# Low halves of the second layer's first MLP weights by an adding DMA, and banks opened without matmuls of zeros

## The chip, the core and the metric

The kernel runs on one core of a Trainium2 chip. In the profile its engines are PE (matmuls; PEld is its weight load), DVE (element by element), ACT (activations and copies), POOL and SP, each with its own queue of instructions in order, and 16 DMA engines move the data. HBM is the large memory, SBUF the working memory of 128 partitions, PSUM the memory with eight banks that matmuls write. The metric is the device time of one execution, in microseconds (us); lower is better.

## What is computed

A trunk of two encoder layers on 256 tokens of 2048 features, all float32. Cut to what matters here:

```python
mod = silu(c) @ w_ada[l] + b_ada[l]              # six vectors: shift, scale, gate, twice
h = _rmsnorm(x) * (1.0 + sc_a) + sh_a
proj = h @ w_in[l]
...                                              # two kinds of attention
x = x + g_a * (concatenate([out_a, out_b]) @ w_o[l])
h = _rmsnorm(x) * (1.0 + sc_m) + sh_m
y = square(relu(h @ w_mlp_in[l])) @ w_mlp_out[l] # 2048 -> 8192 -> 2048
x = x + g_m * y
```

After both layers x is normed once more. The weights of the MLP are 2 x 64 MiB a layer.

## The kernel before

Activations stand with features on the partitions: 16 chunks of 128 features by 256 tokens. A product takes a weight block of 128 x 2048 (1 MiB, all 2048 contraction rows of one tile of 128 output features) and walks its 16 chunks.

**Weights in two halves.** PE's fast float32 form (F32R) keeps fewer bits than float32. So `weights` (L131) loads a block into `raw` on SP's queue (`raw`, L150, five buffers that the modulation's blocks share) and splits it, in two pieces of 1024 columns: ACT rounds `hi` from `raw` (L140), DVE makes `lo = raw - hi` (L141). The activations are split in the same way, so that a product is hi x hi + hi x lo + lo x hi: three matmuls for a chunk. `hi` and `lo` have four buffers each, that is room for two blocks. `weights` also hands out the loads and sums of the modulation (`ada_load`, `ada_sums`): a credit that grows with each block of weights says when the next of 192 modulation blocks is loaded.

**Two forms of product.** `mac` (L173) makes three matmuls of 256 columns. `wide` (L187) has the two parts of the activations side by side and makes one matmul of 512 columns with `hi` (L196) and one of 256 with `lo` (L197) for a chunk; its product is the sum of the bank's two halves, which `joined` (L740) takes: ACT copies one half (L744), DVE adds the other (L745).

**The MLP.** In each of four blocks of 2048 hidden features, `layer` (L696 to L717) makes the first product, tile pair by tile pair, and puts it through `relu2` (L748), then the second product with `update_wide`. The first 12 tiles of the first block come from `norm_then_by_k` (L532), contraction-chunk by contraction-chunk while the norm's chunks appear. In layer 1 the first product uses `wides` (L700): 4 tiles in the first block, 16 in each of the other three, 52 in all. In layer 0 it uses `pair`.

**Banks shared by two tiles.** `by_k` (L218) adds to several tiles by turns, two in a bank. `open_banks` (L209) opens each such bank with a matmul of zeros over all 512 columns (L213), and every later matmul adds. It is called for six banks at each of four norms' products and for two banks at four other places (the later part of the input projection and the start of the output projection, in both layers): 32 matmuls.

**Order.** The program is written in the order of the Python calls; a scheduler then sets the order on each engine, from its own estimate of when things are ready, and puts in the waits. A tile's buffer is given again when its readers are done.

Of the kernel before, what the change touches and what calls it, by code (L numbers as in the profile page):

```python
# [9 lines left out]
F32 = mybir.dt.float32  # L10
# [80 lines left out]

EARLY = {5: (0,), 6: (1, 2)}  # chunk pair of layer 0 -> quarters of w_d's contraction to run behind it
LEAD = 10  # modulation blocks summed ahead of the first norm
WHOLE = 6  # chunk pairs of layer 0's first product in plain float32 passes
# modulation blocks loaded per block of weights: in the two attentions (the second in two stretches),
# in the first products of a layer and in its MLP
RATE_A0, RATE_A1, RATE_A2, RATE_K, RATE_M = 1.1, 0.5, 0.7, 0.6, 0.66
FILL = "lb|0|1|2|3|r"  # setup pieces between the chunk pairs of layer 0


class Trunk:
# [27 lines left out]

# [1 line left out]
    def weights(self, src, width=2048):  # L131
        nc = self.nc
        raw = self.raw(src, width)
        out = []
        half = width // 2
        for i in range(2):
            v = raw[:, i * half : (i + 1) * half]
            hi = self.wp.tile([P, half], F32R, tag="hi", name=self.name("hi"), bufs=4)
            lo = self.wp.tile([P, half], F32R, tag="lo", name=self.name("lo"), bufs=4)
            nc.scalar.activation(hi, v, AF.Copy)  # L140
            ins = nc.vector.tensor_tensor(lo, v, hi.bitcast(F32), ALU.subtract)  # L141
            out.append((hi, lo))
        self.ada_sums(ins)
        self.credit += self.rate
        while self.credit >= 1.0 and self.ada_todo:
            self.credit -= 1.0
            self.ada_load()
        return out

    def raw(self, src, width):  # L150
        raw = self.wp.tile([P, width], F32, tag="raw", name=self.name("raw"), bufs=5)
        self.nc.sync.dma_start(raw, src)
        return raw

    def parts(self, name):
        """Room for a chunk's two parts: each, and both side by side."""
        v = self.u(name, F32R)
        return v[:, 0], v[:, 1], v.rearrange("p a b -> p (a b)")

    def split(self, val, name, wide=False):  # L160
        """[P, 2, T] as two chunks, each in two parts; wide: these side by side."""
        if not wide:
            hi, lo = self.u(name + "h", F32R), self.u(name + "l", F32R)
            self.nc.scalar.activation(hi, val, AF.Copy)
            self.nc.vector.tensor_tensor(lo, val, hi.bitcast(F32), ALU.subtract)
            return [(hi[:, i], lo[:, i]) for i in range(2)]
        out = [self.parts(name) for _ in range(2)]
        for i, (hi, lo, _) in enumerate(out):
            self.nc.scalar.activation(hi, val[:, i], AF.Copy)
            self.nc.vector.tensor_tensor(lo, val[:, i], hi.bitcast(F32), ALU.subtract)  # L170
        return out

    def mac(self, ps, w, c, m, x, first, last):  # L173
        mm = self.nc.tensor.matmul
        hi, lo = w[0][:, c : c + m], w[1][:, c : c + m]
        mm(ps, hi, x[0], start=first, stop=False)  # L176
        mm(ps, hi, x[1], start=False, stop=False)  # L177
        mm(ps, lo, x[0], start=False, stop=last)  # L178

# [6 lines left out]

    def wide(self, src, xs):  # L187
        """A feature tile; its product is the sum of the two halves of the bank."""
        ps = self.bank("ps")
        nk = len(xs)  # L190
        w = self.weights(src, nk * P)
        per = nk // 2
        mm = self.nc.tensor.matmul
        for k, (x, _, both) in enumerate(xs):
            hi, lo = (v[:, (k % per) * P : (k % per) * P + P] for v in w[k // per])
            mm(ps.rearrange("p a b -> p (a b)"), hi, both, start=k == 0, stop=False)  # L196
            mm(ps[:, 0], lo, x, start=False, stop=k == nk - 1)  # L197
        return ps

    def wides(self, srcs, xs):  # L200
        return [self.wide(src, xs) for src in srcs]

# [6 lines left out]
    def open_banks(self, n):  # L209
        """Banks of zeros, open for two tiles to add to by turns."""  # L210
        banks = [self.bank("pk") for _ in range(n)]
        for b in banks:
            self.nc.tensor.matmul(  # L213
                b.rearrange("p a b -> p (a b)"), self.zeros[:, :P], self.zeros, start=True, stop=False
            )
        return banks

    def by_k(self, banks, srcs, xs, k0, nk, n=4, whole=None):  # L218
        """Chunks from k0 of tiles that share banks in pairs; each block has n tiles of each chunk.
        Given the chunks whole, in plain float32 passes."""  # L220
        kpb = srcs[0].shape[-1] // (n * P)
        for b, src in enumerate(srcs):
            width = kpb * n * P
            if whole:
                w = [self.wp.tile([P, n * P], F32, tag=tag, name=self.name("w"), bufs=4) for tag in ("hi", "lo")]
                for i in range(kpb):
# [3 lines left out]
            for i in range(kpb):  # L230
                k = k0 + i
                for j in range(n):
                    tile = n * b + j
                    ps, last = banks[tile // 2][:, tile % 2], k == nk - 1 and tile % 2 == 1
                    c = (i * n + j) * P
                    if whole:
                        self.nc.tensor.matmul(ps, w[i][:, j * P : j * P + P], whole[i], start=False, stop=last)  # L237
                    else:
                        half = width // 2
                        self.mac(ps, w[c // half], c % half, P, xs[k], False, last)  # L240

    def tokens_by_k(self, pss, w, xs, first, last):
        """Token-major: pss[t] += x^T w for the chunks of one block."""
        mm = self.nc.tensor.matmul
# [8 lines left out]
    def small(self, src, xs, n):  # L253
        """n feature tiles, in banks of two, from one block that holds all of a short contraction."""
        w = self.weights(src)
# [14 lines left out]

# [1 line left out]
    def ada_plan(self):  # L272
# [15 lines left out]
    def ada_sums(self, after=None):  # L288
        """Sums over what has been loaded, on VectorE behind an instruction whose data came later."""
        nc = self.nc  # L290
# [32 lines left out]

# [1 line left out]
    def setup(self):  # L325
# [13 lines left out]
        nc.sync.dma_start(self.vec, io["vec"])  # L339
        self.zeros = cp.tile([P, 2 * T], F32R, name="zeros")  # L340
        nc.vector.memset(self.zeros.bitcast(F32), 0.0)
        self.eps = cp.tile([P, 1], F32, name="eps")
# [115 lines left out]

# [1 line left out]
    def sumsq(self, acc, val, alone=False):  # L460
        """Adds val^2, [P, 2, T], to the squares' sums acc; or, alone, puts it beside them."""
        nc = self.nc
# [15 lines left out]
    def rstd(self, acc, n):  # L478
        """1 / rms over n features, on every partition, from the squares' sums."""
        nc = self.nc  # L480
# [18 lines left out]
    def modulated(self, r, k, sh, sc, whole):  # L499
        """Chunks k and k + 1 of the modulated norm of x."""  # L500
        nc = self.nc
# [14 lines left out]
    def latent(self, vals, g):  # L516
        """Weighted rms norm over pairs of feature chunks, split."""
        nc = self.nc
# [13 lines left out]
    def norm_then_by_k(self, l, acc, sh, sc, src, n, nwhole, fill=(), early=()):  # L532
        """The modulated norm of x, and the first 4n feature tiles of its product, of whose
        contraction the first nwhole eighths take plain float32 passes."""
        r = self.rstd(acc, D)
# [17 lines left out]

# [1 line left out]
    def layer(self, l, acc):  # L555
# [140 lines left out]
        for fb in range(NFB):  # L696
            hid = []
            for m in range(0 if fb else 12, NK, 2):
                srcs = [io["w_m1"][l, NK * fb + m + j - 12] for j in range(2)]
                ps = self.wides(srcs, h) if l else self.pair(srcs, h)  # L700
                for b in banks:
# [38 lines left out]
    def joined(self, ps, out):  # L740
        """The sums of the halves of two banks."""
        for i in range(2):
# [10 lines left out]

# [1 line left out]
    def rope_k(self, ps):  # L755
        """Rows 0:64 are the keys, rows 64: their halves swapped; out twice, each over zeros."""
        nc = self.nc
# [23 lines left out]

# [1 line left out]
    def softmax_parts(self, s, least):  # L783
        """exp(max - (-s)) in place of the negated scores, and 1 / its row sums."""
        nc = self.nc
# [103 lines left out]

# [1 line left out]
    def run(self):  # L891
# [86 lines left out]
```

## Time and profile before

| | |
|---|---|
| median of 3 runs | 2266.11 us (2265.44 to 2266.87) |
| profiled execution, first to last instruction (span) | 2262.9 us |
| median less that span | 3.2 us |
| PE, PEld, DVE, ACT, POOL busy | 2202.6, 2018.0, 1654.4, 1110.2, 2.0 us |
| DMA | 585.67 MB, 259 GB/s over the span |

The profile is one execution, taken on the chip. Its page gives the busy time of each engine, the chain of work that ended last (followed back from the last instruction to what released it each time), groups of instructions by line with their number, mean duration and the idle time of the engine before them, and the DMA issues. The trace behind it answers further views: waits (who waited for whom), timelines and busy time in stretches ("PEclk" is the granted share of PE's clock, "DMA share" the mean busy share of the 16 DMA engines). "x104" is a count; "[1.36 <-DVE sum L745]" is idle time of the engine and what ended it. The matmuls' ends are modelled, so where PE's pace matters it is read from counts or starts.

### The profile page before, as it was taken

The page shows a single profiled execution, that of the slowest core. Times are in us where ns is not written, and L with a number is a line of the kernel's source. Part 1 is how long each engine was busy: PE and PEld are TensorE (multiplying, and loading weights), DVE is VectorE, ACT ScalarE, POOL GpSimd, SP SyncE. Part 2 cuts the span into 40 slices and gives each one's busy share as a digit, 9 for nine tenths or more (in the row PEclk, how much of TensorE's full clock was granted, in tenths as well). Part 3 has the DMA queues.
Part 4 walks back from the last instruction along what each step waited for, and adds up shares of the span by engine and source line. Part 5 has one row for each costly group of instructions (what it writes and reads, how often), then busy time and mean ns, then how long its engine had stood idle before and what let it go on. Part 6 is the DMA issues. An engine that isn't in the chain of part 4 may idle for free.

```text
span 2262.9 us, 35366 instructions
## 1 busy us (share of the span) xinstructions
PE 2202.6 (97%) x14508; PEld 2018.0 (89%) x14508; DVE 1654.4 (73%) x2224; ACT 1110.2 (49%) x1608; POOL 2.0 (0%) x10
## 2 busy tenths in 40 slices
PE   3999999999999999999999999999999999999998
PEld 2899889999899899899889998999988888888887
DVE  7889768888877877877888776666655555565565
ACT  2555664355454345345444465534635534544553
POOL 0000000000000000000000000000000000000000
PEclk8999999999999999999999999999999999999999
DMA  9988678898888888887879766664555555555552
GB/s 366 352 318 311 258 279 312 298 341 325 298 310 314 305 313 294 314 316 292 317 256 345 273 226 225 242 228 165 204 189 191 186 194 187 186 187 186 187 188 75
DMA packets 85268, 585.67 MB, mean 259 GB/s; under 512 B 9457, under 2 KB 9841, under 8 KB 20593
## 3 DMA queue, kind: packets, MB, share of 16 engines
q1 hardware_dynamic: 85106, 583.42, 70.9%
q8 instruction: 113, 1.85, 0.3%
q14 instruction: 49, 0.40, 0.0%
HBM read 581.28 MB, written 2.10 MB: 258 GB/s over the span
## 4 chain that ended last, share of the span: by engine, by line
PE 94%; DVE 3%; ACT 1%; DMA 1%; issue 1%; DVEq 0%; SPq 0%; ACTq 0%
PE ps L196 30%; PE ps L197 15%; PE ps L177 7%; PE ps L176 7%; PE ps L178 7%; PE pk L176 5%; PE pk L177 5%; PE pk L178 5%; PE pk L237 3%; DVE ada L293 1%; PE pv L251 1%; PE pv L249 1%; PE pv L250 1%; PE po L832 1%; PE psm L867 1%; PE pom L884 1%
## 5 line engine op out<-in xcount | busy, mean ns | idle before, releaser
L141 DVE TENSOR_TENSOR lo<-raw,hi 128x1024 fp32r<-128x1024 f32 (+1 forms) x728 | 861.4, 1185 | 469.9 <-ACT hi L140 468.1
L140 ACT ACTIVATE hi<-raw 128x1024 fp32r<-128x1024 f32 (+1 forms) x728 | 747.2, 1029 | 907.5 <-PE ps L196 478.0
L196 PE MATMUL ps<-hid,hi 128*128 128x512 f32 x2048 | 717.9, 395 | 0.0
L197 PE MATMUL ps<-hid,lo 128*128 128x256 f32 x2048 | 574.3, 280 | 0.0
L196 PEld LDWEIGHTS ps<-hid,hi 128*128 128x128 f32 x2048 | 383.9, 187 | 90.8 <-DVE hid L170 0.8
L293 DVE SCALAR_TENSOR_TENSOR ada<-ada,cond 128x2048 f32<-128x2048 f32 x192 | 438.0, 2284 | 8.5 <-ACT cond L337 6.8
L197 PEld LDWEIGHTS ps<-hid,lo 128*128 128x128 f32 x2048 | 387.0, 189 | 0.0
L196 PE MATMUL ps<-h,hi 128*128 128x512 f32 x832 | 292.4, 396 | 0.0
L176 PE MATMUL ps<-h,hi 128*128 128x256 f32 x1024 | 291.7, 285 | 0.0
L177 PE MATMUL ps<-h,hi 128*128 128x256 f32 x1024 | 290.5, 284 | 0.0
L178 PE MATMUL ps<-h,lo 128*128 128x256 f32 x1024 | 290.4, 284 | 0.0
L197 PE MATMUL ps<-h,lo 128*128 128x256 f32 x832 | 233.5, 281 | 0.0
L176 PE MATMUL pk<-h,hi 128*128 128x256 f32 x752 | 213.4, 288 | 3.9 <-ACT h L507 3.9
L177 PE MATMUL pk<-h,hi 128*128 128x256 f32 x752 | 214.8, 286 | 0.6 <-DVE h L508 0.6
L178 PE MATMUL pk<-h,lo 128*128 128x256 f32 x752 | 214.6, 286 | 0.0
L176 PEld LDWEIGHTS ps<-h,hi 128*128 128x128 f32 x1024 | 194.7, 190 | 0.4
L177 PEld LDWEIGHTS ps<-h,hi 128*128 128x128 f32 x1024 | 194.7, 190 | 0.4
L178 PEld LDWEIGHTS ps<-h,lo 128*128 128x128 f32 x1024 | 194.7, 190 | 0.2
L196 PEld LDWEIGHTS ps<-h,hi 128*128 128x128 f32 x832 | 156.1, 188 | 37.6
L197 PEld LDWEIGHTS ps<-h,lo 128*128 128x128 f32 x832 | 157.2, 189 | 0.0
L738 DVE SCALAR_TENSOR_TENSOR x<-ps,mod,x 128x256 f32<-128x256 f32 x224 | 108.3, 484 | 59.6 <-PE ps L197 54.9
L176 PEld LDWEIGHTS pk<-h,hi 128*128 128x128 f32 x752 | 145.3, 195 | 5.4 <-ACT h L507 5.3
(211 smaller groups left out, 2677.1 us busy)
## 6 DMA issues: line engine op xcount, KB each, us to landing
raw<-in_w_m SPq DMA_DIRECT2D x232, 1024.0 KB, 4.9
ada<-in_w_ada SPq DMA_DIRECT2D x192, 1024.0 KB, 5.1
raw<-in_w_ob SPq DMA_DIRECT2D x24, 1024.0 KB, 5.1
raw<-in_w_m SPq DMA_DIRECT2D x32, 768.0 KB, 4.5
raw<-in_w_dv SPq DMA_DIRECT2D x16, 1024.0 KB, 4.8
raw<-in_w_a SPq DMA_DIRECT2D x20, 768.0 KB, 6.4
raw<-in_w_t SPq DMA_DIRECT2D x12, 1024.0 KB, 5.0
w<-in_w_a SPq DMA_DIRECT2D x24, 384.0 KB, 5.2
```

Source lines behind the costliest of these rows:

```text
L140: nc.scalar.activation(hi, v, AF.Copy)
L141: ins = nc.vector.tensor_tensor(lo, v, hi.bitcast(F32), ALU.subtract)
L176: mm(ps, hi, x[0], start=first, stop=False)
L177: mm(ps, hi, x[1], start=False, stop=False)
L178: mm(ps, lo, x[0], start=False, stop=last)
L196: mm(ps.rearrange("p a b -> p (a b)"), hi, both, start=k == 0, stop=False)
L197: mm(ps[:, 0], lo, x, start=False, stop=k == nk - 1)
L237: self.nc.tensor.matmul(ps, w[i][:, j * P : j * P + P], whole[i], start=False, stop=last)
L249: mm(ps, xh, hi, start=first and k == 0, stop=False)
L250: mm(ps, xh, lo, start=False, stop=False)
L293: ins = nc.vector.scalar_tensor_tensor(w, w, 1.0, self.cond, ALU.mult, ALU.mult, accum_out=acc[:, i : i + 1])
L738: self.nc.vector.scalar_tensor_tensor(x, ps[i][:, j], g[:, m + i : m + i + 1], x, ALU.mult, ALU.add)
```

## The change

- Layer 1's first MLP product takes its weights from a new function, `weights_added`: ACT writes `hi` as before and, into `lo`, the negated rounded value (the same copy with scale -1); a DMA on POOL's queue then adds `raw` to `lo` in SBUF. DVE has no part in it, and the function neither grows the modulation's credit nor places its sums.
- `hi` and `lo` have six buffers each instead of four, also where `by_k` loads plain float32 blocks into them. The memory for it comes from the tile of zeros and from a smaller scratch for POOL's DMA descriptors (2048 bytes a partition).
- `open_banks` only takes banks. The first matmul of the first tile in each bank has `start=True` instead; a flag turns off the check of matmul groups that share a bank.
- Comments and docstrings go.

```diff
@@ weights
-            hi = self.wp.tile([P, half], F32R, tag="hi", name=self.name("hi"), bufs=4)
-            lo = self.wp.tile([P, half], F32R, tag="lo", name=self.name("lo"), bufs=4)
+            hi = self.wp.tile([P, half], F32R, tag="hi", name=self.name("hi"), bufs=6)
+            lo = self.wp.tile([P, half], F32R, tag="lo", name=self.name("lo"), bufs=6)
@@
+    def weights_added(self, src, width=2048):
+
+        nc = self.nc
+        raw = self.raw(src, width)
+        out = []
+        half = width // 2
+        for i in range(2):
+            v = raw[:, i * half : (i + 1) * half]
+            hi = self.wp.tile([P, half], F32R, tag="hi", name=self.name("hi"), bufs=6)
+            lo = self.wp.tile([P, half], F32R, tag="lo", name=self.name("lo"), bufs=6)
+            nc.scalar.activation(lo, v, AF.Copy, scale=-1.0)
+            nc.scalar.activation(hi, v, AF.Copy)
+            nc.gpsimd.dma_start(lo, v, accum_op=ALU.add)
+            out.append((hi, lo))
+        return out
@@ mac
-    def mac(self, ps, w, c, m, x, first, last):
+    def mac(self, ps, w, c, m, x, first, last, shared=False):
...
-        mm(ps, hi, x[0], start=first, stop=False)
+        mm(ps, hi, x[0], start=first, stop=False, skip_group_check=shared)
...
@@ wide
-        w = self.weights(src, nk * P)
+        w = (self.weights_added if added else self.weights)(src, nk * P)
@@ open_banks
-        banks = [self.bank("pk") for _ in range(n)]
-        for b in banks:
-            self.nc.tensor.matmul(
-                b.rearrange("p a b -> p (a b)"), self.zeros[:, :P], self.zeros, start=True, stop=False
-            )
-        return banks
+
+        return [self.bank("pk") for _ in range(n)]
@@ by_k
-                w = [self.wp.tile([P, n * P], F32, tag=tag, name=self.name("w"), bufs=4) for tag in ("hi", "lo")]
+                w = [self.wp.tile([P, n * P], F32, tag=tag, name=self.name("w"), bufs=6) for tag in ("hi", "lo")]
...
+                    first = k == 0 and tile % 2 == 0
...
-                        self.mac(ps, w[c // half], c % half, P, xs[k], False, last)
+                        self.mac(ps, w[c // half], c % half, P, xs[k], first, last, True)
@@ setup
-        self.zeros = cp.tile([P, 2 * T], F32R, name="zeros")
-        nc.vector.memset(self.zeros.bitcast(F32), 0.0)
@@ layer
-                ps = self.wides(srcs, h) if l else self.pair(srcs, h)
+                ps = self.wides(srcs, h, True) if l else self.pair(srcs, h)
@@ kernel
-    nc = bacc.Bacc("TRN2", target_bir_lowering=False, num_devices=1)
+    nc = bacc.Bacc("TRN2", target_bir_lowering=False, num_devices=1, dynamic_dma_scratch_size=2048)
```

More of the change, by code (lines that the diff above doesn't have):

```diff
@@ L171, in split @@
         return out
-    def mac(self, ps, w, c, m, x, first, last):
+    def mac(self, ps, w, c, m, x, first, last, shared=False):
         mm = self.nc.tensor.matmul
         hi, lo = w[0][:, c : c + m], w[1][:, c : c + m]
-        mm(ps, hi, x[0], start=first, stop=False)
-        mm(ps, hi, x[1], start=False, stop=False)
-        mm(ps, lo, x[0], start=False, stop=last)
+        mm(ps, hi, x[0], start=first, stop=False, skip_group_check=shared)
+        mm(ps, hi, x[1], start=False, stop=False, skip_group_check=shared)
+        mm(ps, lo, x[0], start=False, stop=last, skip_group_check=shared)
     def tile_cols(self, ps, src, xs, m=P):
@@ L185, in tile_cols, with wide @@
             self.mac(ps, w[k // per], (k % per) * m, m, xs[k], k == 0, k == nk - 1)
-    def wide(self, src, xs):
+    def wide(self, src, xs, added=False):
         ps = self.bank("ps")
         nk = len(xs)
-        w = self.weights(src, nk * P)
+        w = (self.weights_added if added else self.weights)(src, nk * P)
         per = nk // 2
@@ L198, in wide, with wides @@
         return ps
-    def wides(self, srcs, xs):
-        return [self.wide(src, xs) for src in srcs]
+    def wides(self, srcs, xs, added=False):
+        return [self.wide(src, xs, added) for src in srcs]
     def pair(self, srcs, xs):
@@ L235, in by_k @@
                     c = (i * n + j) * P
+                    first = k == 0 and tile % 2 == 0
                     if whole:
-                        self.nc.tensor.matmul(ps, w[i][:, j * P : j * P + P], whole[i], start=False, stop=last)
+                        self.nc.tensor.matmul(
+                            ps, w[i][:, j * P : j * P + P], whole[i], start=first, stop=last, skip_group_check=True
+                        )
                     else:
                         half = width // 2
-                        self.mac(ps, w[c // half], c % half, P, xs[k], False, last)
+                        self.mac(ps, w[c // half], c % half, P, xs[k], first, last, True)
     def tokens_by_k(self, pss, w, xs, first, last):
```

## The prediction

> **What bounds the kernel now.** I read the page first (busy time, slices, chain, groups), then TensorE's waits, then stretches of the second layer's MLP, then the timelines there. The page:
>
> ```profile
> PE 2202.6 (97%) x14508; PEld 2018.0 (89%) x14508; DVE 1654.4 (73%) x2224; ACT 1110.2 (49%) x1608; POOL 2.0 (0%) x10
> ...
> PE 94%; DVE 3%; ACT 1%; DMA 1%; issue 1%; DVEq 0%; SPq 0%; ACTq 0%
> ...
> L141 DVE TENSOR_TENSOR lo<-raw,hi 128x1024 fp32r<-128x1024 f32 (+1 forms) x728 | 861.4, 1185 | 469.9 <-ACT hi L140 468.1
> ```
>
> PE is busy 97% of the span of 2262.9 us and is 94% of the chain. DVE's subtractions, part of which the change removes, are the costliest group, but they are DVE's and DVE is 3% of the chain. PE's waits, the longest four:
>
> ```profile
> PE pk L237 <- DMA w<-in_w_a: 18.1, 1, 18.1
> PE pn L486 <- DVE acc L475: 15.3, 1, 15.3
> PE pn L496 <- DVE diag L495: 4.7, 4, 1.6
> PE pk L176 <- ACT h L507: 3.9, 4, 1.2
> ```
>
> None is for `hi` or `lo`, nor is one of the seven behind them (3.6 us and less). The two large ones lie in the first 49 us, the rest at norms and in the attention. So PE's own work sets the time, and no work taken from DVE shortens it. A gain can come only from work taken from PE: the zeros. A loss comes from whatever makes `lo` later than PE asks for it. That is a question of DMA:
>
> ```profile
> core 0: us, PE busy (x) PEld busy (x) DVE busy (x) ACT busy (x) POOL busy (x), PEclk, DMA share, GB/s
> 26.00:48.00 22.00, 4.57 (x15) 3.59 (x15) 20.12 (x33) 6.67 (x13) 0.00 (x0) 0.67 0.99 384
> 1640.00:1700.00 60.00, 60.00 (x348) 52.91 (x347) 36.25 (x44) 23.36 (x22) 0.00 (x0) 1.00 0.57 193
> 1900.00:1960.00 60.00, 60.00 (x341) 52.00 (x341) 32.87 (x43) 34.24 (x53) 0.00 (x0) 1.00 0.53 185
> ```
>
> The third row is first-product work of layer 1, the stage that changes. PE makes 341 matmuls in 60 us, so a feature tile (16 chunks, 32 matmuls) takes 32 x 60 / 341 = 5.63 us. The DMA engines are 0.53 busy bringing one 1 MiB block per tile. The first row is the fastest that they go in this trace: 384 GB/s at a share of 0.99, so 1 MiB (1.049 MB) costs all 16 engines at least 1.049 / 0.384 = 2.73 us.
>
> **The change, part by part.**
>
> *Zeros.* 32 matmuls of 512 columns at L213 go. The pieces of the chain that hold them:
>
> ```profile
> 26.95 2.77 PE pk L213 x6
> ...
> 128.24 0.46 PE pk L213 x2
> ...
> 330.49 0.46 PE pk L213 x2
> ...
> 424.96 0.80 PE pk L213 x3
> ...
> 1244.45 0.23 PE pk L213
> ...
> 1422.40 0.46 PE pk L213 x2
> ...
> 1522.38 1.27 PE pk L213 x5
> ```
>
> The first six stand ahead of the wait of 18.1 us for a load (above) and save nothing. The others on the chain sum to 0.46 + 0.46 + 0.80 + 0.23 + 0.46 + 1.27 = 3.68 us. The other eleven are no part of the chain: PE makes them in the shadow of norms. Part of the 1.27 is lost again, since the matmuls behind it wait for squares. I take 3.5. Bounds: 0, and 26 x 0.23 = 6.0. Against it stands PE's clock: PE is idler in a norm without them, and behind a norm the granted clock already falls:
>
> ```profile
> 1173.00:1176.00 3.00, 2.34 (x11) 2.34 (x12) 3.00 (x9) 1.85 (x5) 0.00 (x0) 0.58 0.68 264
> ```
>
> That dip to 0.58 costs 3 x 0.42 = 1.3 us; one more of its size at each of the three later norms would cost 4. I take 0, as the dips are there with the zeros too.
>
> *ACT.* 104 negated copies are added (52 tiles, two halves). What ACT does now in a pair of first-product tiles:
>
> ```profile
> 1901.58 0.36 ACT L744 ACTIVATE sum<-ps 128x256 f32<-128x256 f32 x1
> 1903.30 0.63 ACT L750 ACTIVATE relu<-sum 128x512 f32<-128x512 f32 x1 [1.36 <-DVE sum L745]
> 1903.84 1.04 ACT L140 ACTIVATE hi<-raw 128x1024 fp32r<-128x1024 f32 x1
> 1904.79 0.62 ACT L751 ACTIVATE relu<-relu 128x512 f32<-128x512 f32 x1
> 1905.43 0.73 ACT L169 ACTIVATE hid<-relu 128x256 fp32r<-128x256 f32 x2
> 1906.27 1.06 ACT L140 ACTIVATE hi<-raw 128x1024 fp32r<-128x1024 f32 x1
> ...
> 1912.89 0.37 ACT L744 ACTIVATE sum<-ps 128x256 f32<-128x256 f32 x1
> ```
>
> A pair lasts 1912.89 - 1901.58 = 11.31 us. Start to start, a 1024-wide copy takes 0.95 (1903.84 to 1904.79). After the change: 8 x 0.95 + two sums 0.73 + 0.54 + 0.64 + 0.84 (starts from 1903.30 on) = 10.35 us. ACT fits with 1 us to spare, and in the new program's order a copy stands behind each sum, where ACT now waits 1.36 us. Cost 0; if ACT lost more than that 1 us in waits, 26 pairs would pay for each further tenth 2.6 us in all.
>
> *DVE.* 104 subtractions go. It is idle between them already: 0.
>
> *More room, order.* Six halves instead of four: `hi` and `lo` can stand three tiles (16.9 us) ahead of PE instead of two. PE never waits for them, so 0. The built program keeps PE's order but for the zeros and small moves in the attention; modulation work ends at 1495 us, before the stage, so the missing calls of it move nothing:
>
> ```profile
> L293 DVE SCALAR_TENSOR_TENSOR ada<-ada,cond x192: 2269/2284/2292, 10.4 to 1495.0; 128x2048 f32<-128x2048 f32 x192
> ```
>
> *The waits that are added.* PE's matmul with `lo` (L197) waits for a DMA's landing instead of DVE; everything on PE is queued behind it. POOL's DMA waits for ACT's copy; behind it on POOL stand only the next of 104 such DMAs. A `raw` buffer, one of five, is now held until that DMA lands, and behind it SP's next load waits. As a delay alone this is covered: a 1 MiB load lands in 4.8 us, and a half's DMA of that order sits inside the 16.9 us lead.
>
> ```profile
> L152 SPq DMA_DIRECT2D raw<-in_w_m x11: 328/328/328, 1903.0 to 1959.5; - x11
> DMA to landing us min/median/max: 4.7/4.8/4.9
> ```
>
> SP needs 0.33 us to issue a DMA. POOL issues none of this data in the trace; it has 5.63 / 2 = 2.8 us for each, eight times SP's price, and I count 0. Above 2.8 us POOL itself would be the bound.
>
> *The adding DMA's rate,* the term that decides. Before shows no adding and no SBUF-to-SBUF transfer. Bounds: below, nothing, if it ran beside the loads; above, several loads of the same bytes. An element is added by reading `raw`, reading `lo` and writing `lo`: two streams in for one out, where a load has one in and one out. By the nearest row (2.73 us for 1 MiB of one stream) a tile's add costs 2 x 2.73 = 5.46 us of all 16 engines. With its load, 5.46 + 2.73 = **8.19 us** of DMA per tile against 5.63 us of PE: 2.56 us late per tile. In each run of 16 tiles three are made ahead, during the product before, which needs no adds; 13 remain, and one of the first run of 4: 3 x 13 + 1 = 40 tiles. 40 x 2.56 = 102 us. I take that value because the add's operands leave no reading with fewer than two streams in.
>
> The Trainium skill ("DMA: Bandwidth & Descriptors", Issuing engines are not separate DMA queues) says that DMAs issued by any engine end on the same 16 engines and interleave; before has one data queue, so no row here shows two. By that rule adds and loads sum as above; without it the adds would cost nothing. The figure of that page of the Trainium skill for the fabric (Where 436 GB/s comes from), 435 GB/s, would make a stream 2.41 us per MiB and the loss 40 x (7.23 - 5.63) = 64 us, a time of 2327, an estimate that no run here shows. The Trainium skill ("Collectives: The Full Stack", The bandwidth ceiling) puts an add in the DMA datapath at half of a copy's rate because of its two reads, which no trace here can show.
>
> *Sum.* 102 - 3.5 = +98.5 us on the profiled execution. Its span is 2262.9, 3.2 below the median of the runs, 2266.11, which holds start and end too. 2266.1 + 98.5 = **2365 us**.
>
> **Rivals.**
>
> *The add costs one stream* (not slower). If the engines read `lo` on the side that writes it, a tile needs 2.73 + 2.73 = 5.46 us, just under PE's 5.63, and no `lo` is late. Then the zeros decide: 2266.1 - 3.5 = 2263. It holds up to (5.63 - 2.73) = 2.90 us per tile's add. For it: the share of 0.53 leaves 0.47 free, and the second product behind needs no adds. Against it: the margin is 3%. Beside that, PE's pace alters without a wait: 348 matmuls in 60 us above, 341 later, 2%. 2% of the 600 us of that MLP is 12 us; I take half of it as what another draw may bring either way, 2258 to 2270.
>
> *The add is dearer* (the adder or POOL's issue is slower than the streams): three streams' worth, 8.19 us per add, 10.92 per tile, 40 x 5.29 = 212 us: 2475. Nothing in the trace speaks for or against.
>
> *Reads and writes overlap in part,* 1.5 streams: 6.83 per tile, 40 x 1.20 = 48: 2311.
>
> *The change misses its mark:* fewer DVE instructions bring nothing, as PE waits for none of them. It is part of every case.
>
> **How the numbers follow.** Two streams 0.40 (its own range 2320 to 2400), one stream 0.32, dearer 0.20, in part 0.08. A measurement of this kernel can tell some 0.2% (4.5 us) from no change. The one-stream case centres on -3.5, so of its 0.32 I give 0.15 to faster, 0.15 to the same and 0.02 to slower. Slower: 0.40 + 0.20 + 0.08 + 0.02 = 0.70. The range reaches from the one-stream case (2259) into the dearer one (2480); a tenth is left out above, a few hundredths below.
>
> **What would show it.** Right: PE waits for `ps` L197 <- the DMA into `lo`, some 30 us in each of three stretches of 16 first-product tiles, which last about 120 us instead of 90; DMA share near 1 there; the `lo` DMAs take longer to land than 16.9 us; the second product as before; no L213 rows. Wrong: a DMA share clearly below 1 in those stretches with no wait at L197 (one stream), or PE waiting there with the engines idle (then POOL or latency is the bound).

## The result, and the profile after

| | before | after |
|---|---|---|
| median | 2265.78 us (2260.61 to 2266.87) | 2351.34 us (2349.04 to 2352.95) |
| profiled execution (span) | 2262.9 us | 2349.6 us |

The changed kernel takes 1.0377 times as long, interval 1.0364 to 1.0390: **85.6 us slower**. The forecast was 2365 us. The sign, the stage and the mechanism are as forecast; three sizes are off.

The page of the kernel after (engines, queues, the chain by engine and by line, three groups, the new DMA):

```profile
PE 2221.3 (95%) x14476; PEld 2015.0 (86%) x14476; DVE 1531.2 (65%) x2119; ACT 1205.6 (51%) x1712; POOL 92.1 (4%) x114
...
q1 hardware_dynamic: 85106, 583.42, 67.4%
q0 software_dynamic: 14976, 54.53, 11.8%
...
PE 78%; DMA 11%; DVE 6%; issue 3%; ACT 1%; POOL 0%; DVEq 0%; POOLq 0%; ACTq 0%
...
L141 DVE TENSOR_TENSOR lo<-raw,hi 128x1024 fp32r<-128x1024 f32 (+1 forms) x624 | 733.2, 1179 | 385.6 <-ACT hi L140 380.6
...
L213 PE MATMUL ps<-h,lo 128*128 128x256 f32 x832 | 241.9, 291 | 59.9 <-DMA lo<-raw 59.5
...
L213 PEld LDWEIGHTS ps<-h,lo 128*128 128x128 f32 x832 | 158.4, 190 | 81.7 <-DMA lo<-raw 81.4
...
lo<-raw POOLq DMA_DIRECT2D x104, 512.0 KB, 16.5
```

DVE has 123 us less work, and that bought nothing: PE was the bound. PE counts 18.7 us more of busy time with 32 matmuls fewer, part of it in longer records in the stage that changed (L213: 291 ns on average; 281 for the same matmuls, L197, before). DMA, 1% of the chain before, is now 11%. L213 is in this kernel the matmul with `lo` in `wide`, and the idle time in front of it, 59.5 us on PE and 81.4 on its weight load, is put down to the adding DMA. The last line says that a half takes 16.5 us from issue to landing. PE's longest waits after (total, times, longest):

```profile
PE ps L213 <- DMA lo<-raw: 59.5, 59, 2.4
PE pk L249 <- DMA w<-in_w_a: 18.6, 1, 18.6
PE pn L498 <- DVE acc L487: 15.3, 1, 15.3
PE pn L508 <- DVE diag L507: 9.8, 5, 2.7
```

The first line is new; the second and third are nearly those of before. Fifty-nine short waits, and the weight loads in front of the matmuls wait beside them, are the print of a supply that is a little too slow for each tile, not of one late transfer. Where this happens, in stretches of layer 1 (busy time and count of each engine, then granted clock, DMA share, GB/s):

```profile
core 0: us, PE busy (x) PEld busy (x) DVE busy (x) ACT busy (x) POOL busy (x), PEclk, DMA share, GB/s
1720.00:1740.00 20.00, 20.00 (x114) 17.23 (x113) 2.06 (x5) 16.10 (x21) 5.69 (x8) 1.00 1.04 251
1749.60:1809.70 60.10, 49.52 (x260) 39.31 (x259) 6.44 (x16) 41.35 (x57) 14.19 (x17) 1.00 1.05 281
1723.00:1837.00 114.00, 96.19 (x513) 77.95 (x512) 18.25 (x36) 74.82 (x103) 23.48 (x28) 1.00 1.02 270
1837.00:1927.00 90.00, 90.00 (x511) 77.88 (x510) 48.20 (x60) 40.68 (x42) 3.45 (x4) 1.00 0.66 216
```

The third row is one first product of 16 tiles: 512 matmuls in 114 us, at a DMA share of 1.02 (0.53 in the first-product stretch of before that the prediction shows). The first row is its beginning: PE runs without a gap on the tiles made ahead, while the DMA engines are already full. The second row is the steady state behind it: 260 matmuls in 60.1 us, that is 32 x 60.1 / 260 = 7.4 us a tile instead of 5.63. The fourth row is the second product, some 90 us as before, with DMA to spare. The clock is 1.00 in all four, so it is not the clock.

Which transfers fill the engines there, by queue (the DMA view of the kernel after, 1740 to 1810 us: packets, MB, share of 16 engines):

```profile
DMA packets 4016, 19.47 MB, mean 278 GB/s; under 512 B 445, under 2 KB 445, under 8 KB 2839
...
q0 software_dynamic: 2695, 9.81, 70.7%
q1 hardware_dynamic: 1317, 9.61, 34.1%
```

For the same bytes the adds (q0) take twice the time of the loads (q1). In 70 us, 0.707 x 70 = 49.5 us for 9.81 MB is 5.29 us per tile (1.049 MB) of adds, and 0.341 x 70 = 23.9 us for 9.61 MB is 2.60 us per tile of loads. The shares sum to 1.05: records on an engine overlap a little. 9.81 MB in 70 us is a tile each 7.5 us, which is what PE's count shows.

The length of the whole stage can be read from one row of each kernel, the first and last start of the matmul with `lo`; before, then after:

```profile
L197 PE MATMUL ps<-h,lo x832: 277/280/284, 1598.6 to 2160.6; 128*128 128x256 f32 x167
```
```profile
L213 PE MATMUL ps<-h,lo x832: 274/281/579, 1603.1 to 2247.6; 128*128 128x256 f32 x167
```

562.0 us before, 644.5 after: 82.5 of the 86.7 us between the spans lie here. Another 4.5 are there when the stage begins (1598.6 against 1603.1), in spite of the zeros that went; 0.3 are won back behind it. By the starts of the first matmul of each product, the four first-product runs (4, 16, 16, 16 tiles) took 22.6, 88.7, 90.4 and 90.5 us before and 29.1, 114.3, 115.8 and 113.6 after: +6.5, +25.6, +25.4, +23.1, in sum **80.6**.

### The profile page after: what moved, and what is told of

It reads as the page before. It is cut to its first block, busy times and chain, and to the rows that moved or that the text cites. A ratio compares the mean times of both kernels' runs of the same rounds, so it can differ in the third digit from the quotient of the medians.

```text
span 2349.6 us, 35538 instructions
## 1 busy us (share of the span) xinstructions
PE 2221.3 (95%) x14476; PEld 2015.0 (86%) x14476; DVE 1531.2 (65%) x2119; ACT 1205.6 (51%) x1712; POOL 92.1 (4%) x114
## 3 DMA queue, kind: packets, MB, share of 16 engines
q0 software_dynamic: 14976, 54.53, 11.8%
## 4 chain that ended last, share of the span: by engine, by line
PE 78%; DMA 11%; DVE 6%; issue 3%; ACT 1%; POOL 0%; DVEq 0%; POOLq 0%; ACTq 0%
PE ps L212 22%; PE ps L213 11%; DMA lo<-raw 11%; PE ps L193 7%; PE ps L192 7%; PE ps L194 7%; PE pk L192 4%; PE pk L193 4%; PE pk L194 4%; DVE ada L307 3%; PE pv L263 1%; PE pv L265 1%; PE pv L264 1%; PE psm L879 1%; DVE lo L141 1%
## 5 line engine op out<-in xcount | busy, mean ns | idle before, releaser
L140 ACT ACTIVATE hi<-raw 128x1024 fp32r<-128x1024 f32 (+1 forms) x624 | 635.5, 1023 | 816.1 <-PE ps L212 394.6
L141 DVE TENSOR_TENSOR lo<-raw,hi 128x1024 fp32r<-128x1024 f32 (+1 forms) x624 | 733.2, 1179 | 385.6 <-ACT hi L140 380.6
L213 PE MATMUL ps<-hid,lo 128*128 128x256 f32 x2048 | 574.1, 280 | 0.0
L213 PEld LDWEIGHTS ps<-hid,lo 128*128 128x128 f32 x2048 | 386.9, 189 | 0.0
L213 PE MATMUL ps<-h,lo 128*128 128x256 f32 x832 | 241.9, 291 | 59.9 <-DMA lo<-raw 59.5
L212 PE MATMUL ps<-h,hi 128*128 128x512 f32 x832 | 297.8, 399 | 0.0
L194 PE MATMUL ps<-h,lo 128*128 128x256 f32 x1024 | 290.7, 284 | 0.0
L213 PEld LDWEIGHTS ps<-h,lo 128*128 128x128 f32 x832 | 158.4, 190 | 81.7 <-DMA lo<-raw 81.4
L161 ACT ACTIVATE hi<-raw 128x1024 fp32r<-128x1024 f32 x104 | 110.0, 1058 | 86.7 <-PE ps L212 80.6
## 6 DMA issues: line engine op xcount, KB each, us to landing
lo<-raw POOLq DMA_DIRECT2D x104, 512.0 KB, 16.5
```

What stands on the lines that cost most here:

```text
L194: mm(ps, lo, x[0], start=False, stop=last, skip_group_check=shared)
```

## The experiments

Two questions. Is the loss in that stage the adds' rate on engines that they share with the loads (the theory), or the adds' delay, POOL's issue or ACT's extra copies (rivals)? And where do the 4.5 us ahead of it come from?

**The same program with a copy in place of the add.** A copying DMA reads one stream in and writes one out; all waits, queues and ACT's copies stay.

```diff
-            nc.gpsimd.dma_start(lo, v, accum_op=ALU.add)
+            nc.gpsimd.dma_start(lo.bitcast(F32), v)
```

> The same DMAs on POOL, from raw into lo, that copy instead of adding (the low half is then the whole weight, so that part of the computation is changed). Rate (each add is two streams through engines that are full): a copy is one stream, half of the add's 5.33 us per tile; 2.73 + 2.67 = 5.4 us of DMA per tile against 5.63 of PE, so the loss nearly goes: 2263 to 2280 us, PE's wait for lo under 10 us in all, a 4096-byte packet near 160 ns instead of 328. Rival, delay or POOL (the way over POOL and a DMA is too long or POOL's issue too slow, whatever moves): as the changed kernel, 2350. Rival, ACT (the second copy): 2350 too, with no waits for a DMA.

2268.21 us (2263.94 to 2274.39), ratio 1.0016, interval 1.0005 to 1.0028. PE waits for `lo` once, 0.6 us, and its weight loads 1.9 us in all. From the page of this kernel, and one of its 16-tile stretches:

```profile
q0 software_dynamic: 14976, 54.53, 5.9%
```
```profile
1713.00:1801.00 88.00, 88.00 (x509) 76.93 (x508) 17.55 (x36) 73.85 (x102) 14.27 (x27) 1.00 0.98 357
```

The same packets and bytes as after take 5.9% of the span instead of 11.8%: 0.059 x 2265.4 / 52 = 2.57 us a tile against 0.118 x 2349.6 / 52 = 5.33 for the add. An add takes what two copies take, measured; that its two reads are the reason is not shown by the time alone. (The edit also makes the DMA's destination plain float32 where the add's is F32R, and no run parts the two.) At one stream the engines are 0.98 busy and PE waits for nothing in that stretch: the rival of the prediction in which the add costs one stream would indeed have come out near the time of before, and its margin was as thin as it said. ACT makes all its 104 extra copies here, and the first run lasts 22.9 us against 22.6: their cost is 0.3 us at most. The Trainium skill ("Collectives: The Full Stack", The bandwidth ceiling) gives the adding DMA half of a copy's rate, for its two reads; in the rate, 5.33 against 2.57 agrees.

**Half the dose.** The add for the first tile of each pair, DVE's subtraction for the other.

```diff
-        return [self.wide(src, xs, added) for src in srcs]
+        return [self.wide(src, xs, added and i == 0) for i, src in enumerate(srcs)]
```

> Adds in every other tile of the same product, DVE's subtractions in the rest. Rate: a pair of tiles needs 2 x 2.73 + 5.33 = 10.8 us of DMA against 11.3 of PE, under the limit, so almost the whole loss goes, not half: 2266 to 2280. Rival, delay per add (each add late by itself): half the loss stays, some 2308. Rival, ACT: half too.

2270.83 us (2266.88 to 2274.07), ratio 1.0025, interval 1.0010 to 1.0039. A 16-tile stretch (window) of this kernel:

```profile
1719.00:1809.00 90.00, 89.66 (x511) 77.90 (x510) 33.91 (x49) 62.15 (x89) 11.22 (x13) 1.00 0.96 269
```

Half of the adds cost none of the 80 us: the same program without any add, further down, takes 2270.87. A price per add would have left half of it; what is left is a rate, which costs nothing as long as the engines keep up. A pair needs 5.3 + 2 x 2.6 = 10.5 us of DMA and gives PE 11.3 us of work, so they do, at a share of 0.96.

**The adds alone on the engines.** Each run loads one block and uses it for all its tiles, so that the products of that run are those of one block; all adds, copies and matmuls stay.

```diff
-        raw = self.raw(src, width)
+        if self.kept is None:
+            self.kept = self.raw(src, width)
+        raw = self.kept
...
-            hid = []
+            hid, self.kept = [], None
```

> All adds stay, but each run of first-product tiles of layer 1 loads one block of weights and uses it for all its tiles (the product is then that of repeated weights), so 48 loads go. Rate, loads and adds sharing the engines: 5.33 us of DMA per tile against 5.63, the loss goes: 2263 to 2285, the share of the DMA engines in those runs still near 0.95, the landing of an add well under 16.5 us. Rival, adds slow or late by themselves, beside the loads: 2350 stays.

2271.00 us (2265.6 to 2277.58), ratio 1.0022, interval 1.0008 to 1.0035. A 16-tile stretch of this kernel, and its adds' queue on the page:

```profile
1719.00:1809.00 90.00, 90.00 (x512) 78.00 (x511) 17.98 (x36) 74.52 (x102) 23.71 (x28) 1.00 0.92 195
```
```profile
q0 software_dynamic: 14976, 54.53, 12.2%
```

An add is as dear as after (0.122 x 2274.7 / 52 = 5.34 us a tile), but beside no loads it fits into 5.63 us, and PE waits for adds 2.2 us in all, none of it in this stretch. POOL issues as many, 0.86 us each, and ACT copies as much, so neither is the bound: what makes the loss is adds and loads together on one set of engines. The Trainium skill ("DMA: Bandwidth & Descriptors", Issuing engines are not separate DMA queues) says that DMAs of all issuers end on the same 16 engines; the shares of the two queues after, 70.7% and 34.1%, agree.

**Less room.** After with four halves of each kind, as before the change; the same edit in `weights_added` and in `by_k`.

```diff
-            hi = self.wp.tile([P, half], F32R, tag="hi", name=self.name("hi"), bufs=6)
-            lo = self.wp.tile([P, half], F32R, tag="lo", name=self.name("lo"), bufs=6)
+            hi = self.wp.tile([P, half], F32R, tag="hi", name=self.name("hi"), bufs=4)
+            lo = self.wp.tile([P, half], F32R, tag="lo", name=self.name("lo"), bufs=4)
```

> The changed kernel with four halves of hi and lo instead of six. Rate: the engines are as full as before, only one tile less is made ahead in each run: 4 x 2.4 = 10 us more, some 2360. Rival, delay (the 16.5 us to landing against the lead): the lead falls from 16.9 to 11.3 us and every tile pays for it, 52 x some 2 to 5 us more, over 2450.

2370.91 us (2369.36 to 2377.06), ratio 1.0475, interval 1.0454 to 1.0495. That is nearly 20 us over after: no delay of a whole landing per tile, but twice what the rate theory had said. In the profiled execution the four first-product runs take 26.7 us longer than after, and the stage begins 7.5 us earlier. PE's wait here, and the stage's row:

```profile
PE ps L213 <- DMA lo<-raw: 71.2, 52, 4.1
```
```profile
L213 PE MATMUL ps<-h,lo x832: 274/280/582, 1596.1 to 2265.0; 128*128 128x256 f32 x167
```

The 16-tile runs last 120.7, 124.1 and 121.4 us, 7.5 more than after for one tile of room. The steady pace is the same (the window from 1750 to 1810 us has 257 matmuls at a share of 1.05, with a granted clock of 0.94 that the full engines hide). So a tile of room is not worth the 1.9 us by which a tile is late, but nearly the whole 7.5 us of a tile's DMA. The reason that I put to a test next: in steady state the DMA engines work without a pause, so a stretch lasts as long as the tiles whose adds fall into it, plus a fixed end.

**More room.** Seven halves. The memory comes from one of five `raw` buffers, so the changed kernel with four `raw` buffers and six halves is its base (both with a scratch of 1024 bytes). The first edit is in both, also for the two other tiles that share the room of `raw`; the second in the kernel with seven alone, at all its places.

```diff
-        raw = self.wp.tile([P, width], F32, tag="raw", name=self.name("raw"), bufs=5)
+        raw = self.wp.tile([P, width], F32, tag="raw", name=self.name("raw"), bufs=4)
```
```diff
-            hi = self.wp.tile([P, half], F32R, tag="hi", name=self.name("hi"), bufs=6)
-            lo = self.wp.tile([P, half], F32R, tag="lo", name=self.name("lo"), bufs=6)
+            hi = self.wp.tile([P, half], F32R, tag="hi", name=self.name("hi"), bufs=7)
+            lo = self.wp.tile([P, half], F32R, tag="lo", name=self.name("lo"), bufs=7)
```

> The changed kernel with four raw buffers instead of five (and the scratch of 1024 bytes), the base for the run with seven halves. Both theories: the loads are not late in the stretches, since the DMA engines and not the loads' lead set the pace there, so the 16-tile stretches stay at 114 to 116 us; the total within 6 us of the changed kernel's.

> The changed kernel with seven hi and lo buffers instead of six, and four raw buffers instead of five to make the room. Theory (the lead is eaten while the engines already work on the next adds: a 16-tile stretch lasts 2 x 5.63 us plus 8.06 us, add 5.33 and load 2.73, for each tile that found no room ahead): 116.0 us with room for three tiles, 124.1 with two (121 to 124 measured with four halves), and 112.0 with three and a half: 4 us less a stretch, 12 us less in all than the run with six halves and four raw buffers. Rival (the engines just need 7.6 us a tile, and a tile of lead saves only the 1.95 us by which it is late): 114.8 against 115.8 us, 3 us less in all.

Base 2354.61 us (2348.3 to 2361.83), ratio 1.0397, interval 1.0376 to 1.0419; seven halves 2349.85 us (2349.62 to 2353.49), ratio 1.0379, interval 1.0365 to 1.0393. The 16-tile runs of the base last 115.0, 116.3 and 114.5 us, with seven halves 111.9, 113.2 and 111.5: 3.1 less each, between the 4 of the theory and the 1 of the rival. PE's waits with seven halves:

```profile
PE ps L213 <- DMA lo<-raw: 50.1, 43, 2.1
...
PE ps L212 <- DVE hid L186: 7.0, 4, 2.3
```

The four runs together are 12.4 us shorter, yet the medians differ by 4.8, and their intervals overlap: the second line is new, 7.0 us, and the second products that follow lasted 5 us longer in sum (92.5, 92.8 and 90.1 us against 89.0, 90.6 and 90.5). Part of what the room gains is given back there, and the stage begins 5.7 us later (1605.9 against 1600.2 us): as a whole, half a tile more of room is not shown to gain anything.

What room does can be read from when the first add of a 16-tile run is issued: some 6 us ahead of the run's first matmul with four halves, 11.7 after, 14.1 with seven. That lead and the run's length together are 125 to 128 us in all twelve runs of these four kernels but one (130.1, with four halves). So the adds of 16 tiles take nearly the same time on full engines, and room sets how early they begin: a tile of it lets them begin 5.8 us earlier, most of the 7.5.

As a fit, three tiles of PE (3 x 5.63 = 16.9 us) plus 7.5 us for each tile without room ahead give 121.9 us with two tiles of room (122.1 measured, mean of three), 114.4 with three (114.6; 115.3 in the base), 110.7 with three and a half (112.2). The form is the prediction's at three tiles of room (16 x 5.63 + 13 x excess is the same sum). The theory on record for seven halves, two tiles of PE and 8.06 us, gives 124.1, 116.0 and 112.0, and not the steady 7.5 us of the windows.

The time to landing is not what costs: in the base with four `raw` buffers, an add lands in 10.6 us, and a 16-tile run is as long as after, where it lands in 16.5.

```profile
L162 POOL DMA_DIRECT2D lo<-raw x104: 859/862/1007, 1591.8 to 2228.2; - x104
...
DMA to landing us min/median/max: 4.4/10.6/13.4
```

**ACT's copies alone.** Before, with ACT writing the negated copy into `lo` ahead of DVE, which then writes over it.

```diff
+            if twice:
+                nc.scalar.activation(lo, v, AF.Copy, scale=-1.0)
             nc.scalar.activation(hi, v, AF.Copy)
```

> The kernel before, in whose first product of layer 1 ACT writes the negated copy into lo as well, before DVE writes lo as ever: ACT's added work alone. Forecast: it fits with 1 us a pair to spare, 2266. Rival, ACT is part of the loss: up to 26 pairs by some us, 2290.

2269.14 us (2266.49 to 2272.71), ratio 1.0019, interval 1.0010 to 1.0027. The run of 4 tiles lasts 27.4 us instead of 22.6; the 16-tile runs are unchanged. The granted clock in that run is 0.94, which makes 1.6 of the 4.8 us; that the rest is the wait of DVE's subtraction behind the added copy is argued. The copying DMA above has the same copies and no such cost.

**Everything but the adds.** After, with the first products of layer 1 on `weights`.

```diff
-                ps = self.wides(srcs, h, True) if l else self.pair(srcs, h)
+                ps = self.wides(srcs, h) if l else self.pair(srcs, h)
```

> The changed kernel with DVE's subtractions back in layer 1: the zeros gone and six halves, no adding DMA. The forecast's terms without the add: 2265.9 - 3.5 = 2262.4. Rival, order: six halves let ACT and DVE split weights further ahead, in front of work that the attention and the norms wait for, as the changed kernel's 4.5 us of lateness at the start of the second layer's MLP suggests: 2268 to 2271.

2270.87 us (2265.93 to 2275.38), ratio 1.0022, interval 1.0013 to 1.0030: 5.1 us slower than before, as the rival had it and not the forecast's terms. So the adds are 2351.34 - 2270.87 = **80.5 us**, and the rest is no gain.

**The zeros alone:** after without the adds and with four halves and the scratch of before.

```diff
-                ps = self.wides(srcs, h, True) if l else self.pair(srcs, h)
+                ps = self.wides(srcs, h) if l else self.pair(srcs, h)
...
-            hi = self.wp.tile([P, half], F32R, tag="hi", name=self.name("hi"), bufs=6)
-            lo = self.wp.tile([P, half], F32R, tag="lo", name=self.name("lo"), bufs=6)
+            hi = self.wp.tile([P, half], F32R, tag="hi", name=self.name("hi"), bufs=4)
+            lo = self.wp.tile([P, half], F32R, tag="lo", name=self.name("lo"), bufs=4)
...
-    nc = bacc.Bacc("TRN2", target_bir_lowering=False, num_devices=1, dynamic_dma_scratch_size=2048)
+    nc = bacc.Bacc("TRN2", target_bir_lowering=False, num_devices=1)
```

> The zeros alone gone, four halves, no add. Forecast: 3.5 us less, 2262.4. Rival, shadow: they cost nothing, as the norms' chains hide them or PE's clock takes the gain back: 2266.

**Six halves alone:** before with the zeros kept, also in `by_k`, and a smaller scratch to make room.

```diff
-            hi = self.wp.tile([P, half], F32R, tag="hi", name=self.name("hi"), bufs=4)
-            lo = self.wp.tile([P, half], F32R, tag="lo", name=self.name("lo"), bufs=4)
+            hi = self.wp.tile([P, half], F32R, tag="hi", name=self.name("hi"), bufs=6)
+            lo = self.wp.tile([P, half], F32R, tag="lo", name=self.name("lo"), bufs=6)
...
-    nc = bacc.Bacc("TRN2", target_bir_lowering=False, num_devices=1)
+    nc = bacc.Bacc("TRN2", target_bir_lowering=False, num_devices=1, dynamic_dma_scratch_size=1024)
```

> Six halves alone, zeros kept, no add. Forecast: 0, 2266. Rival, order: 3 to 8 us more, 2269 to 2274, in the attention and at the norms.

Without zeros 2263.90 us (2260.06 to 2267.77), ratio 0.9991, interval 0.9983 to 1.0000; six halves 2271.77 us (2268.74 to 2274.02), ratio 1.0027, interval 1.0015 to 1.0038. The sum, -1.8 + 6.0 = +4.2, is the 5.1 us of the run before within what can be told. The zeros' gain can hardly be told from none; for the six halves the rival's 3 to 8 us came true. Without zeros, PE's wait for `diag` at the norms, 4.7 us in the prediction, becomes

```profile
PE pn L508 <- DVE diag L507: 7.3, 4, 2.7
```

Of this, 2.3 us lie at the first norm, ahead of the long wait for a load, where they cost nothing. At the three later norms all of PE's waits together (for DVE and ACT) grow from 7.9 to 10.8 us, so nearly 3 us of what PE no longer does becomes waiting.

**The scratch alone,** to hold it apart from the halves:

```diff
-    nc = bacc.Bacc("TRN2", target_bir_lowering=False, num_devices=1)
+    nc = bacc.Bacc("TRN2", target_bir_lowering=False, num_devices=1, dynamic_dma_scratch_size=1024)
```

> The kernel before, with the smaller scratch for POOL's descriptors (1024 bytes a partition, as in the run with six halves only) and nothing else. Theory (the 6 us of that run are the six halves'): as the kernel before, within 1.5 us. Rival (the smaller scratch costs them): 2269 to 2273 us.

2263.68 us (2259.87 to 2267.52), ratio 0.9998, interval 0.9989 to 1.0007: the scratch costs nothing, the halves cost the 6 us. The input projection with the attention behind it, in layer 0 and layer 1, first of this kernel (four halves), then with six halves:

```profile
177.40:330.30 152.90, 147.38 (x901) 130.78 (x899) 126.40 (x220) 88.93 (x168) 0.00 (x0) 1.00 0.76 281
1275.40:1422.90 147.50, 147.49 (x901) 131.31 (x899) 108.32 (x198) 87.32 (x165) 0.00 (x0) 1.00 0.63 229
```
```profile
176.10:332.50 156.40, 151.34 (x901) 134.06 (x899) 130.67 (x225) 89.77 (x169) 0.00 (x0) 0.97 0.78 287
1275.40:1425.40 150.00, 147.90 (x901) 131.19 (x899) 106.60 (x197) 89.53 (x168) 0.00 (x0) 1.00 0.62 223
```

The same 901 matmuls take 3.5 us more in layer 0 and 2.5 more in layer 1. In layer 1 PE, which waited for nothing, now does (that window's waits with six halves):

```profile
PE psc L801 <- ACT k L268: 1.6, 1, 1.6
PE psm L867 <- DVE sm L869: 0.5, 1, 0.5
```

This repeats: the stretch of layer 1 takes 147.3 to 147.5 us in all five kernels with four halves, and 149.9 to 150.0 in all seven with six. That ACT and DVE make weights further ahead, in front of work that the attention waits for, is argued from whose waits these are; no run put the order back with six halves.

The 3.5 us of layer 0 are another matter. PE waits no longer there with six halves (5.0 us against 5.5), but it is busy 4 us longer with the same work at a granted clock of 0.97. Four halves give 152.5 to 153.4 us there. Six give 155.7 to 156.8 in five kernels, with a clock of 0.97 to 0.99; 154.8 with the copying DMA, at 1.00; and less than four halves do in the kernel with four `raw` buffers:

```profile
177.20:328.00 150.80, 147.41 (x900) 131.03 (x899) 130.44 (x225) 91.34 (x171) 0.00 (x0) 1.00 0.80 296
```

So the cost in layer 0 comes mostly with a lower clock, and six halves do not always bring it. Nor may the two stretches simply be added up to the 6 us: of the 7.0 us between these two profiled executions 3.7 are there when the second layer's MLP begins, and the other 3.3 are PE's pace in that MLP, where it waits for nothing in either.

## Why the prediction was right, and where its sizes were off

- **What bounds the kernel:** right. 123 us less of DVE gave nothing, as no wait for `lo` was there to remove.
- **The add is two streams on shared engines:** right in the price and the sharing, shown three ways: the copy halves it and the loss goes (2.57 against 5.33 us), half the adds cost none of it, and the adds without loads fit. It was taken at 5.46 us. That its two reads make the price is the prediction's reason, which no run tests by itself, apart from the type that the DMA writes or from the memory that it reads and writes.
- **The sum of a tile, "5.46 + 2.73 = 8.19 us of DMA per tile":** the step that was mis-sized. Measured: 5.29 + 2.60 = 7.89 us of records, which overlap by 5%, so a tile each 7.5 us. The excess over PE is 1.87 us, not 2.56. It is a small difference of two large numbers, so 8% of the sum is 27% of the loss: 40 x 1.87 = 75 us, not 102. The 2.73 was the mean of the busiest stretch of before; beside the adds a load took 2.60. The prediction's row of the stage itself (185 GB/s at a share of 0.53) gives 1.049 x 0.53 / 0.185 = 3.0 us, which would have made the forecast worse: 135 us. Its lower estimate, 7.23 us a tile and 64 us, fell short. The rivals' other prices fell: one stream (2263), part overlap (2311), the dearer adder or POOL's issue (2475).
- **"Three are made ahead ... 13 remain, and one of the first run of 4":** right for the 16-tile runs (3 x 13 x 1.87 = 73 us, 74.1 measured), wrong for the run of 4, which lost 6.5 us instead of one excess. Its first add is issued 8.4 us ahead of its first matmul, not 11.7 as in the others, and the adds of two tiles have landed there, not of three. The granted clock in this run is 0.94, which makes some 1.7 us (0.06 x 29.1). How the rest divides between rate and landing stays open; the copying DMA, which lands sooner, loses 0.3 us there, and the adds without loads 2.6.
- **ACT, POOL, DVE:** 0 each, right. The copies cost 0.3 us at most in the run of 4 with the copying DMA, an issue by POOL 0.86 us against the bound of 2.8.
- **Zeros, -3.5:** -1.8, interval -3.9 to 0. The sum of the chain's rows was counted almost whole; nearly 3 us came back as waits at the three later norms. The rows away from the norms (0.46 + 0.46 + 0.23 + 0.46 = 1.6 us) come near what was gained, but no run took them out alone.
- **"PE never waits for them, so 0" for six halves:** wrong, +6.0 us (interval 3.4 to 8.6). It looked only at who waits for `hi` and `lo`. The waits that came, 2.1 us in layer 1's attention, are for other work of ACT and DVE; for the rest the runs show a lower clock in layer 0 and no cause that repeats.
- **The sum:** +102 - 3.5 + 0 forecast; +80.5 - 1.8 + 6.0 = +84.7 by the runs, 85.6 measured. That 2365 is only 14 us off is in part luck: the adds were forecast 21.5 us too dear, while the halves' 6.0 us were missing and the zeros' gain was put 1.7 us too high.

The prediction also named a sign: the DMAs into `lo` landing later than the lead of 16.9 us. The row of the adding DMA (minimum, median and maximum of its issue in ns, then of its landing) has that only at the upper end. The median lies just below, and the runs with four `raw` buffers and with four halves lose as much or more with medians of 10.6 and 9.3 us. So this was no sign of the loss:

```profile
L162 POOL DMA_DIRECT2D lo<-raw x104: 862/862/1010, 1594.5 to 2226.5; - x104
...
DMA to landing us min/median/max: 4.4/16.5/19.8
```

## What to carry to other kernels

Before work is moved from an engine that is not the bound to the DMA engines, add up what each tile then needs of all 16 of them, with an add in SBUF counted as two copies, and compare it with the time that the bound engine spends on a tile: here it was free below (shares of 0.92 to 0.98), and above it every tile that could not be made ahead paid the difference. Such a difference of large numbers is only as good as the price of a stream, and these traces have no single one: by its records a MiB of load took 3.15 us in before (1740 to 1810 us, 55% busy), 2.70 in its busiest stretch, 3.06 beside the copies and 2.60 beside the adds. A forecast from such a price needs a range of that width. More buffers are not free even where memory is: six halves cost 6.0 us here, part of it as waits for other work of ACT and DVE. No version here beats the kernel before by more than can be told; the nearest is that without the zeros alone.

## What the runs showed that was not expected

- POOL needs 0.86 us to issue an adding DMA of 128 x 1024, and 0.53 us for a copying one (medians of 104 each), where SP needs 0.33 for a load.
- The DMA share can stand above 1 (1.05 in the steady state): records of one engine must overlap there, and the share alone does not say how much of it is work.
- PE has two paces without a wait and at the full granted clock: a 16-tile run of before lasts 88.7 or 90.5 us, and it changes from one product to the next. 2% of a stage is therefore not an edit's doing until it repeats.
